# Turned blocks in a Mamba-2 / gated-MLP layer: two buffers and another order in the SSD part, landing in place in the latent part

## The chip, the cores and the metric

The kernel runs on one core of a Trainium2 chip. The metric is device time in microseconds of one execution. A comparison goes by the median of several executions; the profile is of one more execution, taken by the hardware profiler, with a time of its own.

## The reference

One layer over 256 latent tokens with a prefix of 256 context tokens, width 2048, all in float32. In short:

```
shift, scale, gate = split(silu(c) @ w_ada + b_ada)          # and the same for the context
h = rmsnorm(tokens, g_pre) * (1 + scale) + shift
z = h @ w_in              # x, B, C, dt for all 512 tokens; z_ssd, u, v, z_mlp for the 256 latents
xbc = silu(depthwise_conv5(z[:4096] channels))               # 2048 of x, 1024 of B, 1024 of C
y = bidirectional SSD scan(x, dt, A, B, C), chunks of 128, 8 groups of 4 heads;
    the latents' scans start from the context's final states
y_a = rmsnorm((y + d_skip * x) * silu(z_ssd), g_ssd)
y_b = rmsnorm(u * (w_s . rmsnorm(v, g_v) + b_s) * silu(z_mlp), g_mlp)
out = x + gate * rmsnorm(concat(y_a, y_b) @ w_out, g_post)
```

In a group of the scan, products such as `states = B^T (decay * dt * x)` contract over tokens, so x and B are needed with tokens in the partitions, while the projection leaves them with channels in the partitions: a block must be turned.

## The kernel before, in words

**Products in three parts.** Every large weight arrives as float32 and is split into hi (rounded, ScalarE) and lo = w - hi (VectorE), in halves of 128 x 1024 (lines 84 to 89; in the SSD part by `split_hi` and `split_lo`, lines 540 to 550). TensorE then does hi x hi, hi x lo and lo x hi. The pool of halves holds four hi and four lo.

**Stages.** (1) Up to about 122 us: adaLN, norms, the first seven channel tiles and dt. (2) To about 450 us: the remaining 25 of 32 channel tiles (`REST`, line 24), 48 matmuls each, of 512 columns for x and B tiles and 256 for C tiles. The tiles go by groups: of group g, tiles 4g and 4g+1 are x, 4g+2 is B, 4g+3 is C. While TensorE does later tiles, the finished ones are convolved and their group's SSD products are done. (3) To about 820 us: 16 blocks of 512 columns for the latents (v, u, z_mlp, z_ssd, four each), and what is computed from them. (4) The output projection in two halves, then the last norm and the output.

**The planner.** In stage 2 and in the first block of stage 3 the order of instructions on TensorE, VectorE, ScalarE and GpSimd is the order in which the program writes them (`manual_schedule`). Steps are written through `later(dt, fn)`, line 578, which puts a step into a queue with a due time, and `pump(dt)`, line 582, which moves the planner's clock on by dt and writes all steps that are due. `pump` is called after every six matmuls: with 1.3 for tiles of 512 columns, 0.65 for tiles of 256. So the due times decide the order and nothing else; on the chip an instruction starts when its engine is free and its inputs are there. SP, which issues the DMAs, is ordered by the framework, as are all engines from the second latent block on (line 1218 ends the manual part).

**One group in stage 2** (`plan_tile`, line 972). After a tile is done come its convolution and silu, then:
- x and B are turned, for group 0 by TensorE (`ptx`, `ptb`, into PSUM, and a copy by ScalarE) and for the others by `turn` and `turned` (lines 738 and 745): VectorE turns 32 x 32 squares into a tile T (tag `tt`, one buffer for x's two turns and B's), SP stores T to a scratch in DRAM (`Dx`, `Db`, two buffers), and four loads on SP bring it back to `xk` or `bk` with the squares in place. For group 7 B and y go by TensorE too, x does not. `LAND`, 4.5, is the time that the planner leaves for a landing.
- `ssd_w` (line 780): six products on GpSimd, x by decay and dt, into `xw` (four) and `xl` (two); `ssd_sk` two more, d_skip by x, into y, due 3 later.
- Once C is there and `late` more: `ssd_cb` (matmul `pcb`), `ssd_states` (matmuls `psc` from bk and xw, `psl` from bk and xl, lines 865 and 868), then `hs` (`ssd_hc`, `ssd_hd`, `ssd_hl`), `ssd_m`, `ssd_o` (matmul `pso`, line 917), `ssd_yo`, `ssd_ya`, `ssd_yd` (matmul `psy`). `late` is 8 for groups 1 to 6, but 10 for groups 1 and 3.
- y is turned back the same way: `ssd_yc` (T and store `Dy`), `ssd_yt` (loads into `yz`) and `ssd_yf` (line 966, VectorE adds yz to y).
- For the next group, `ssd_d`, `ssd_min` and `ssd_e` make the decay matrix E from R; after the second minimum GpSimd's queue issues the load of the next R (`row_load`, line 721).

**y** is one tile of 128 x 2 x 2048 (token half, channel). Before the scan its eight segments of 512 serve as scratch (`yseg`).

**The latents' turned blocks** (stage 3, z_mlp as kind 2 and z_ssd as kind 3). `lat_z` multiplies block j4 of `vt` or y with silu(z) and squares it for the norm. `lat_t` (line 1110) turns squares into T with VectorE and moves each square into place with 16 DMAs on GpSimd's queue, into a second tile Z; T and Z share a pool of two buffers (tag `gw`, also used by `lat_vn`). `lat_split` (line 1123) scales four parts of Z by g_mlp or g_ssd and splits them into hi and lo, for the output projection. They are due 1.5 and 17 to 20 after the block's end; a block is 20.8 long on the planner's clock.

Of the kernel before, what the change touches and what calls it, by code (L numbers as in the profile page):

```python
# [8 lines left out]
F32 = mybir.dt.float32  # L9
# [6 lines left out]
P = 128  # L16
D = 2048
# [3 lines left out]
NGRP = 8  # L21
# [26 lines left out]
def tile_hybrid_ssd_mlp(  # L48
# [46 lines left out]
    ypool = ctx.enter_context(mkpool(name="ypool", bufs=1, side="right"))  # L95
    y = ypool.tile([P, 2, D], F32, tag="big16", name="y")
    st = ExitStack()
# [56 lines left out]
    def yseg(j):  # L154
        return y[:, j // 4, (j % 4) * 512 : (j % 4 + 1) * 512]

# [8 lines left out]
    s2 = yseg(4)[:, 0:256]  # L165
    at = y[:, 0, 256:512].rearrange("p (t h) -> p t h", t=4)
    fold = yseg(7)[:, 256:320]
# [348 lines left out]
    drp = ctx.enter_context(mkpool(name="drp", bufs=1, space=bass.MemoryType.DRAM))  # L516
    drt = ctx.enter_context(mkpool(name="drt", bufs=2, space=bass.MemoryType.DRAM))
    cv1 = cvs.enter_context(mkpool(name="cv1", bufs=1))
# [216 lines left out]
    def by_pe(g, what):  # L735
        return g == 0 or g == NGRP - 1 and what != "x"

# [12 lines left out]
    def ssd_x(g, xi):  # L750
        S = gs_.setdefault(g, {})
        if xi == 0:
            S["xk"] = cv2.tile([P, 2, 4, P], F32, tag="xk", name=f"xk{g}")
        xt = done.pop(4 * g + xi)
        if not by_pe(g, "x"):
            T = cv1.tile([P, 512], F32, tag="tt", name=f"tx{g}{xi}")
            S["Dx", xi] = turn(T, xt, f"x{g}{xi}")
            return
        p = spt([P, 4, P], f"ptx{g}{xi}")
        for t in range(4):  # L760
            nc.tensor.transpose(p[:, t, :], xt[:, t * P : (t + 1) * P], ident)
        S["ptx", xi] = p

    def ssd_xc(g, xi):
        xk = gs_[g]["xk"][:, xi]
        if by_pe(g, "x"):
# [13 lines left out]
    def ssd_w(g):  # L780
        S = gs_[g]
        h4 = slice(4 * g, 4 * g + 4)
        xw = cv1.tile([P, 2, 2, 256], F32, tag="xw", name=f"xw{g}")
        for t in range(2):
            for d in range(2):
                nc.gpsimd.tensor_tensor(hx(xw[:, t, d, :]), xtok_(g, t), hb(wctx(t, d)[:, h4]), op=ALU.mult)
        xl = cv1.tile([P, 2, 256], F32, tag="xl", name=f"xl{g}")
        for d in range(2):
            nc.gpsimd.tensor_tensor(hx(xl[:, d, :]), xtok_(g, 2 + d), hb(wlt(d)[:, h4]), op=ALU.mult)
        S["xw"], S["xl"] = xw, xl  # L790

    def ssd_b(g):
        bt = done[4 * g + 2]
        S = gs_.setdefault(g, {})
        S["bk"] = cv1.tile([P, 4, P], F32, tag="bk", name=f"bk{g}")
        if not by_pe(g, "b"):
            T = cv1.tile([P, 512], F32, tag="tt", name=f"tb{g}")
            S["Db"] = turn(T, bt, f"b{g}")
            return
        p = spt([P, 4, P], f"ptb{g}")  # L800
        for t in range(4):
            nc.tensor.transpose(p[:, t, :], bt[:, t * P : (t + 1) * P], ident)
        S["ptb"] = p
# [101 lines left out]
    def yg(g, c):  # L905
        return y[:, c, g * 256 : (g + 1) * 256]

# [58 lines left out]
    def ssd_yf(g):  # L966
        ya = y[:, :, g * 256 : (g + 1) * 256]
        nc.vector.tensor_tensor(ya, ya, gs_[g]["pty"].rearrange("p c q k -> p c (q k)"), op=ALU.add)
# [83 lines left out]
    def open_lat():  # L1052
# [3 lines left out]
        gsp = gs.enter_context(mkpool(name="gsp", bufs=1))  # L1056
        L_["vt"] = L_["big"].tile([P, 2, D], F32, tag="b16", name="vt")
        L_["cb2"] = gsp.tile([P, D], F32, name="cb2")
# [51 lines left out]
    def lat_t(kind, j4):  # L1110
        src = L_["vt"] if kind == 2 else y
        cols = slice(j4 * 512, (j4 + 1) * 512)
        T = L_["lt2"].tile([P, 1024], F32, tag="gw", name=f"T{kind}{j4}").rearrange("p (t j c) -> p t j c", t=2, j=4)
        for tk in range(2):
            nc.vector.transpose(T[:, tk].rearrange("p j c -> p (j c)"), src[:, tk, cols])
        Z = L_["lt2"].tile([P, 1024], F32, tag="gw", name=f"Z{kind}{j4}")
        L_["Z"] = Z = Z.rearrange("p (t j c) -> p t j c", t=2, j=4)
        for a in range(4):
            for b in range(4):
                nc.gpsimd.dma_start(Z[32 * b : 32 * b + 32, :, :, 32 * a : 32 * a + 32].rearrange("p t j c -> p (t j) c"),  # L1120
                                T[32 * a : 32 * a + 32, :, :, 32 * b : 32 * b + 32].rearrange("p t j c -> p (t j) c"))

    def lat_split(kind, j):
        src = L_["Z"][:, :, j % 4]
        if kind == 2:
            gcol, hi, lo = C_GMLP, hhi[j][:, 0:256], hlo[j][:, 0:256]
        else:
            gcol, hi, lo = C_GSSD, L_["yah"][:, j, :], L_["yal"][:, j, :]
        hi, lo = (t.rearrange("p (t c) -> p t c", t=2) for t in (hi, lo))
        gc = pc[:, gcol + j : gcol + j + 1]  # L1130
        nc.scalar.mul(hi, src, gc)
        nc.vector.scalar_tensor_tensor(lo, src, gc, hi.bitcast(F32), op0=ALU.mult, op1=ALU.subtract)

    def lat_v(j4, pa):
        cols = slice(j4 * 512, (j4 + 1) * 512)
        for tk in range(2):
            nc.scalar.copy(L_["vt"][:, tk, cols], pa[tk])
            sqj = L_["lt2"].tile([P, 512], BF16, tag="sqj", name=f"sqv{j4}{tk}")
# [4 lines left out]
    def lat_vn(j4):  # L1143
# [5 lines left out]
        for tk in range(2):  # L1149
            vb = L_["vt"][:, tk, cols]  # L1150
            nc.vector.scalar_tensor_tensor(vb, vb, rr[:, 0, tk : tk + 1], gvb, op0=ALU.mult, op1=ALU.mult)
        L_["ws"] = ws

    def lat_sg(j4):
        ws = L_["ws"]
        L_["sg"] = []
        for tk in range(2):
            p = spt([P, 512], f"psg{j4}{tk}")
            for gi in range(4):
                g = 4 * j4 + gi  # L1160
                nc.tensor.matmul(p[:, gi * P : (gi + 1) * P], lhsT=ws[:, gi, :],
                                 rhs=L_["vt"][:, tk, g * P : (g + 1) * P], start=True, stop=True)
            L_["sg"].append(p)

    def lat_u(j4, pa):
        for tk in range(2):
# [26 lines left out]
    for blk in range(16):  # L1193
# [243 lines left out]
```

## Time and profile before

| | us |
|---|---|
| Median of three executions (976.14 to 978.86) | 978.4 |
| The profiled execution | 974.69 |
| Its span, first to last instruction | 972.8 |
| TensorE busy in it | 955.7 |
| VectorE busy | 685.6 |
| ScalarE busy | 482.8 |
| GpSimd busy | 198.6 |

In the rows of the profile, PE is TensorE's matmuls, PEld its weight loads, DVE is VectorE, ACT ScalarE, POOL GpSimd and SP the engine that issues most DMAs (SPq its queue). A row of the timeline gives start, length, engine, line, operation, output<-inputs, shape, count (a row with x4 covers four instructions in a row), and in brackets how long the engine had stood idle and what ended that. Float32 matmuls without the split count as two records each. A row of waits gives total, number and longest. Names are those of the program's tiles without their numbers, so `bk<-Db` is a load of the turned B of any group. "L549" is line 549 of the kernel before; the printed functions carry the same numbers.

### The profile page before, as it was taken

What the parts mean: (1) busy time and instruction counts of PE and PEld (TensorE: products, weight loads), DVE (VectorE), ACT (ScalarE), POOL (GpSimd) and SP (SyncE); (2) the same over time, 40 slices, a digit from 0 to 9 for tenths busy, and PEclk for the clock granted to TensorE, in tenths of its full rate; (3) what the DMA queues carried; (4) which work ended last, traced back from release to release, by engine and by line L of the source; (5) the groups of instructions that cost most, each with busy time, mean ns of one, the idle gap of its engine ahead of it and who ended that gap; (6) DMA issues with size and microseconds to landing.
All of it is one profiled execution on the core that took longest, in us unless ns stands there. A gap on an engine that the chain in (4) does not pass through costs nothing.

```text
span 972.8 us, 13786 instructions
## 1 busy us (share of the span) xinstructions
PE 955.7 (98%) x5138; PEld 771.8 (79%) x5138; DVE 685.6 (70%) x1101; ACT 482.8 (50%) x731; POOL 198.6 (20%) x290
## 2 busy tenths in 40 slices
PE   9999999998997999999999999999999999999997
PEld 4688888786785878787888888887888888888885
DVE  6888798878985868676767776767666665445636
ACT  4344458564662544455445433465565564346612
POOL 0000002522551233354000000043334541000000
PEclk9999999999999999999999999999999999999999
DMA  9999956567676666575877868686556665556722
GB/s 363 417 415 415 365 224 165 149 182 158 138 189 169 147 172 149 160 217 209 295 304 281 289 254 314 259 305 210 200 195 222 223 233 192 212 177 251 266 87 86
DMA packets 145666, 225.09 MB, mean 231 GB/s; under 512 B 114992, under 2 KB 115248, under 8 KB 122944
## 3 DMA queue, kind: packets, MB, share of 16 engines
q1 hardware_dynamic: 138816, 206.55, 62.6%
q0 software_dynamic: 6208, 16.85, 5.4%
q8 instruction: 40, 0.66, 0.3%
q10 hardware_dynamic: 576, 0.82, 0.2%
q14 instruction: 26, 0.21, 0.1%
HBM read 211.02 MB, written 8.98 MB: 226 GB/s over the span
## 4 chain that ended last, share of the span: by engine, by line
PE 87%; DMA 6%; DVE 4%; ACT 1%; SPq 1%; issue 1%; DVEq 0%; ACTq 0%
PE pa L1212 12%; PE pa L1214 12%; PE pa L1213 12%; PE psx L141 8%; PE psx L142 8%; PE psx L143 8%; PE pm L1255 3%; PE pm L1254 3%; PE pm L1253 3%; DMA ada<-in_wada_dram 3%; PE pq L1255 2%; PE pq L1254 2%; PE pq L1253 2%; PE psc L865 2%; PE pso L917 1%; DMA wst<-in_wst_dram 1%
## 5 line engine op out<-in xcount | busy, mean ns | idle before, releaser
L88 DVE TENSOR_TENSOR lo_w<-w,hi_w 128x1024 fp32r<-128x1024 f32 x173 | 210.7, 1222 | 148.8 <-ACT hi_w L87 148.7
L87 ACT CAST hi_w<-w 128x1024 fp32r<-128x1024 f32 x173 | 182.2, 1053 | 220.7 <-PE pa L1214 147.9
L1212 PE MATMUL pa<-hi_w,hhi 128*128 128x512 f32 x512 | 201.2, 393 | 0.0
L1213 PE MATMUL pa<-lo_w,hhi 128*128 128x512 f32 x512 | 199.4, 390 | 0.0
L1214 PE MATMUL pa<-hi_w,hlo 128*128 128x512 f32 x512 | 199.4, 389 | 0.0
L141 PE MATMUL psx<-hhi,hi_w 128*128 128x512 f32 (+1 forms) x400 | 151.5, 379 | 0.0
L143 PE MATMUL psx<-hhi,lo_w 128*128 128x512 f32 (+1 forms) x400 | 145.8, 364 | 0.0
L142 PE MATMUL psx<-hlo,hi_w 128*128 128x512 f32 (+1 forms) x400 | 145.7, 364 | 0.0
L1212 PEld LDWEIGHTS pa<-hi_w,hhi 128*128 128x128 f32 x512 | 96.2, 188 | 20.9 <-issue 1.6
L1214 PEld LDWEIGHTS pa<-hi_w,hlo 128*128 128x128 f32 x512 | 96.1, 188 | 20.0
L1213 PEld LDWEIGHTS pa<-lo_w,hhi 128*128 128x128 f32 x512 | 96.2, 188 | 19.8 <-issue 0.2
L624 DVE SCALAR_TENSOR_TENSOR xbc<-psx,pc,xbc 128x248 f32<-128x248 f32 (+1 forms) x204 | 83.4, 473 | 19.7 <-ACT xbc L608 19.0
L549 DVE TENSOR_TENSOR lo_w<-w,hi_w 128x1024 fp32r<-128x1024 f32 x61 | 81.8, 1349 | 20.0 <-ACT hi_w L543 20.0
L1120 POOL DMA_DIRECT2D Z<-T x128 | 73.7, 583 | 97.2 <-ACT sq L1188 33.0
L141 PEld LDWEIGHTS psx<-hhi,hi_w 128*128 128x128 f32 x400 | 75.5, 189 | 14.4 <-issue 3.1
L142 PEld LDWEIGHTS psx<-hlo,hi_w 128*128 128x128 f32 x400 | 75.6, 189 | 12.9 <-issue 1.7
L143 PEld LDWEIGHTS psx<-hhi,lo_w 128*128 128x128 f32 x400 | 75.5, 189 | 12.2
L543 ACT CAST hi_w<-w 128x1024 fp32r<-128x1024 f32 x61 | 63.6, 1045 | 42.5 <-PE psx L142 29.5
L1253 PE MATMUL pm<-hi_w,hhi 128*128 128x512 f32 x128 | 49.8, 389 | 0.0
L1255 PE MATMUL pm<-hi_w,hlo 128*128 128x512 f32 x128 | 49.8, 389 | 0.0
L1254 PE MATMUL pm<-lo_w,hhi 128*128 128x512 f32 x128 | 49.8, 389 | 0.0
L378 ACT CAST hi_st<-wst 128x448 fp32r<-128x448 f32 (+2 forms) x26 | 17.2, 679 | 57.0 <-DMA wst<-in_wst_dram 57.0
(274 smaller groups left out, 1407.6 us busy)
## 6 DMA issues: line engine op xcount, KB each, us to landing
w<-in_wlat_dram SPq DMA_DIRECT2D x64, 1024.0 KB, 4.8
w<-in_wout_dram SPq DMA_DIRECT2D x32, 1024.0 KB, 4.8
w<-in_wxbc_dram SPq DMA_DIRECT2D x25, 1024.0 KB, 5.6
ada<-in_wada_dram SPq DMA_DIRECT2D x24, 1024.0 KB, 14.0
gate<-in_wada_dram SPq DMA_DIRECT2D x16, 1024.0 KB, 5.0
ada<-in_wada_dram SPq DMA_DIRECT2D x16, 512.0 KB, 12.5
R<-acs POOLq DMA_DIRECT2D x8, 1024.0 KB, 7.0
wst<-in_wst_dram SPq DMA_DIRECT2D x15, 480.0 KB, 13.0
```

The lines of the kernel that those rows point to most:

```text
L87: nc.scalar.copy(hi, raw)
L88: nc.vector.tensor_tensor(lo, raw, hi.bitcast(F32), op=ALU.subtract)
L141: nc.tensor.matmul(ps, lhsT=whi, rhs=hhi[k][:, s], start=start, stop=False)
L142: nc.tensor.matmul(ps, lhsT=whi, rhs=hlo[k][:, s], start=False, stop=False)
L143: nc.tensor.matmul(ps, lhsT=wlo, rhs=hhi[k][:, s], start=False, stop=stop)
L624: nc.vector.scalar_tensor_tensor(ao, zi, cw[:, k : k + 1], ao, op0=ALU.mult, op1=ALU.add)
L1212: nc.tensor.matmul(pa[tk], lhsT=hhi[k][:, t], rhs=whi[:, w], start=k == 0, stop=False)
L1213: nc.tensor.matmul(pa[tk], lhsT=hhi[k][:, t], rhs=wlo[:, w], start=False, stop=False)
L1214: nc.tensor.matmul(pa[tk], lhsT=hlo[k][:, t], rhs=whi[:, w], start=False, stop=k == KT - 1)
L1253: nc.tensor.matmul(p, lhsT=yh[:, t], rhs=whi[:, w], start=j == 0, stop=False)
L1254: nc.tensor.matmul(p, lhsT=yh[:, t], rhs=wlo[:, w], start=False, stop=False)
L1255: nc.tensor.matmul(p, lhsT=yl[:, t], rhs=whi[:, w], start=False, stop=hf == 0 and j == 15)
```

## The change

Five things, by place:
- **Layout.** y and vt become 128 x 4 x 2 x 512 (block, token half, column), so that a block of 512 columns of both halves is contiguous in a partition. Every use is rewritten to the same elements.
- **SSD, buffers.** T (tag `tt`) moves to a pool of two buffers, the scratch in DRAM from two to four.
- **SSD, products.** `ssd_w` keeps the four products of xw; the two of xl become `ssd_wl`, due 3 later, and `ssd_sk` is due 6 after `ssd_w`, where x goes by DMA.
- **SSD, order.** `late` is at least 11 instead of 8 (14 for tile 15, so group 3), `ssd_yt` is due 3 later and `ssd_yf` 4 later after the y product. Of group 7, the second x tile goes by TensorE.
- **Latents.** The 16 DMAs write into the block they came from; Z is gone. The four scales of a block are copied into a small tile first, over a copy of four columns of the newest weight half; the splits read scales from there and are due 23 to 23.3 after the block's end.

```diff
-    y = ypool.tile([P, 2, D], F32, tag="big16", name="y")
+    y = ypool.tile([P, 4, 2, 512], F32, tag="big16", name="y")
...
     def yseg(j):
-        return y[:, j // 4, (j % 4) * 512 : (j % 4 + 1) * 512]
+        return y[:, j % 4, j // 4]
...
-    drt = ctx.enter_context(mkpool(name="drt", bufs=2, space=bass.MemoryType.DRAM))
+    drt = ctx.enter_context(mkpool(name="drt", bufs=4, space=bass.MemoryType.DRAM))
...
     def by_pe(g, what):
-        return g == 0 or g == NGRP - 1 and what != "x"
+        return g == 0 or g == NGRP - 1 and what != "x0"
...
-        if not by_pe(g, "x"):
-            T = cv1.tile([P, 512], F32, tag="tt", name=f"tx{g}{xi}")
+        if not by_pe(g, f"x{xi}"):
+            T = cv2.tile([P, 512], F32, tag="tt", name=f"tx{g}{xi}")
...
+        S["xw"] = xw
+
+    def ssd_wl(g):
+        h4 = slice(4 * g, 4 * g + 4)
         xl = cv1.tile([P, 2, 256], F32, tag="xl", name=f"xl{g}")
         for d in range(2):
             nc.gpsimd.tensor_tensor(hx(xl[:, d, :]), xtok_(g, 2 + d), hb(wlt(d)[:, h4]), op=ALU.mult)
-        S["xw"], S["xl"] = xw, xl
+        gs_[g]["xl"] = xl
...
-            T = cv1.tile([P, 512], F32, tag="tt", name=f"tb{g}")
+            T = cv2.tile([P, 512], F32, tag="tt", name=f"tb{g}")
...
-        lx, lb, ly = (0.7 if by_pe(g, w) else LAND for w in "xby")
+        lx, lb, ly = (0.7 if by_pe(g, w) else LAND for w in (f"x{r}", "b", "y"))
         if lx == LAND:
             tw = max(tw, 2 * LAND + 3)
         if lb == LAND:
-            late = max(late, 8.0)
+            late = max(late, 14.0 if i == 15 else 11.0)
...
         if r == 1:
+            late_w = lx == LAND
             later(d0 + tx + tw, lambda: ssd_w(g))
-            later(d0 + tx + tw + 3, lambda: ssd_sk(g))
+            later(d0 + tx + tw + (3 if late_w else 0), lambda: ssd_wl(g))
+            later(d0 + tx + tw + (6 if late_w else 3), lambda: ssd_sk(g))
...
-                          (16.9 + td + (1.7 if ly < 1 else LAND), ssd_yt), (18.6 + td + (0.7 if ly < 1 else 2 * LAND + 2), ssd_yf)]:
+                          (16.9 + td + (1.7 if ly < 1 else LAND + 3), ssd_yt), (18.6 + td + (0.7 if ly < 1 else 2 * LAND + 6), ssd_yf)]:
...
     def lat_t(kind, j4):
-        src = L_["vt"] if kind == 2 else y
-        cols = slice(j4 * 512, (j4 + 1) * 512)
-        T = L_["lt2"].tile([P, 1024], F32, tag="gw", name=f"T{kind}{j4}").rearrange("p (t j c) -> p t j c", t=2, j=4)
+        src = (L_["vt"] if kind == 2 else y)[:, j4]
+        T = L_["lt2"].tile([P, 1024], F32, tag="gw", name=f"T{kind}{j4}").rearrange("p (u c) -> p u c", c=P)
         for tk in range(2):
-            nc.vector.transpose(T[:, tk].rearrange("p j c -> p (j c)"), src[:, tk, cols])
-        Z = L_["lt2"].tile([P, 1024], F32, tag="gw", name=f"Z{kind}{j4}")
-        L_["Z"] = Z = Z.rearrange("p (t j c) -> p t j c", t=2, j=4)
+            nc.vector.transpose(T[:, 4 * tk : 4 * tk + 4].rearrange("p u c -> p (u c)"), src[:, tk])
+        dst = src.rearrange("p t (j c) -> p (t j) c", c=P)
         for a in range(4):
             for b in range(4):
-                nc.gpsimd.dma_start(Z[32 * b : 32 * b + 32, :, :, 32 * a : 32 * a + 32].rearrange("p t j c -> p (t j) c"),
-                                T[32 * a : 32 * a + 32, :, :, 32 * b : 32 * b + 32].rearrange("p t j c -> p (t j) c"))
+                nc.gpsimd.dma_start(dst[32 * b : 32 * b + 32, :, 32 * a : 32 * a + 32],
+                                    T[32 * a : 32 * a + 32, :, 32 * b : 32 * b + 32])
 
     def lat_split(kind, j):
-        src = L_["Z"][:, :, j % 4]
+        src = (L_["vt"] if kind == 2 else y)[:, j // 4, :, (j % 4) * P : (j % 4 + 1) * P]
+        if j % 4 == 0:
+            L_["gc"] = L_["lt2"].tile([P, 4], F32, tag="gc", name=f"gc{kind}{j}")
+            gcol = (C_GMLP if kind == 2 else C_GSSD) + j
+            nc.vector.tensor_copy(L_["gc"], halves[max(halves)][0][:, 0:4].bitcast(F32))
+            nc.vector.tensor_copy(L_["gc"], pc[:, gcol : gcol + 4])
...
-        gc = pc[:, gcol + j : gcol + j + 1]
+        gc = L_["gc"][:, j % 4 : j % 4 + 1]
         nc.scalar.mul(hi, src, gc)
         nc.vector.scalar_tensor_tensor(lo, src, gc, hi.bitcast(F32), op0=ALU.mult, op1=ALU.subtract)
...
             for jj in range(4):
-                later(17 + jj, lambda kind=kind, j=4 * j4 + jj: lat_split(kind, j))
+                later(23 + 0.1 * jj, lambda kind=kind, j=4 * j4 + jj: lat_split(kind, j))
```

More of the change, by code (lines that the diff above doesn't have):

```diff
@@ L165, in tile_hybrid_ssd_mlp @@
     s2 = yseg(4)[:, 0:256]
-    at = y[:, 0, 256:512].rearrange("p (t h) -> p t h", t=4)
+    at = yseg(0)[:, 256:512].rearrange("p (t h) -> p t h", t=4)
     fold = yseg(7)[:, 256:320]
@@ L765, in ssd_xc @@
         xk = gs_[g]["xk"][:, xi]
-        if by_pe(g, "x"):
+        if by_pe(g, f"x{xi}"):
             nc.scalar.copy(xk, gs_[g]["ptx", xi])
@@ L905, in yg @@
     def yg(g, c):
-        return y[:, c, g * 256 : (g + 1) * 256]
+        return y[:, g // 2, c, (g % 2) * 256 : (g % 2 + 1) * 256]
     def ssd_sk(g):
@@ L966, in ssd_yf @@
     def ssd_yf(g):
-        ya = y[:, :, g * 256 : (g + 1) * 256]
+        ya = y[:, g // 2, :, (g % 2) * 256 : (g % 2 + 1) * 256]
         nc.vector.tensor_tensor(ya, ya, gs_[g]["pty"].rearrange("p c q k -> p c (q k)"), op=ALU.add)
@@ L1056, in open_lat @@
         gsp = gs.enter_context(mkpool(name="gsp", bufs=1))
-        L_["vt"] = L_["big"].tile([P, 2, D], F32, tag="b16", name="vt")
+        L_["vt"] = L_["big"].tile([P, 4, 2, 512], F32, tag="b16", name="vt")
         L_["cb2"] = gsp.tile([P, D], F32, name="cb2")
@@ L1110, in lat_t @@
     def lat_t(kind, j4):
[L1111 to L1113 removed]
+        src = (L_["vt"] if kind == 2 else y)[:, j4]
+        T = L_["lt2"].tile([P, 1024], F32, tag="gw", name=f"T{kind}{j4}").rearrange("p (u c) -> p u c", c=P)
         for tk in range(2):
[L1115 to L1117 removed]
+            nc.vector.transpose(T[:, 4 * tk : 4 * tk + 4].rearrange("p u c -> p (u c)"), src[:, tk])
+        dst = src.rearrange("p t (j c) -> p (t j) c", c=P)
         for a in range(4):
             for b in range(4):
[L1120 to L1121 removed]
+                nc.gpsimd.dma_start(dst[32 * b : 32 * b + 32, :, 32 * a : 32 * a + 32],
+                                    T[32 * a : 32 * a + 32, :, 32 * b : 32 * b + 32])
     def lat_split(kind, j):
[L1124 removed]
+        src = (L_["vt"] if kind == 2 else y)[:, j // 4, :, (j % 4) * P : (j % 4 + 1) * P]
[4 more added lines that the diff above has]
+            nc.vector.tensor_copy(L_["gc"], pc[:, gcol : gcol + 4])
         if kind == 2:
[L1126 removed]
+            hi, lo = hhi[j][:, 0:256], hlo[j][:, 0:256]
         else:
[L1128 removed]
+            hi, lo = L_["yah"][:, j, :], L_["yal"][:, j, :]
         hi, lo = (t.rearrange("p (t c) -> p t c", t=2) for t in (hi, lo))
[L1130 removed]
+        gc = L_["gc"][:, j % 4 : j % 4 + 1]
         nc.scalar.mul(hi, src, gc)
@@ L1134, in lat_v @@
     def lat_v(j4, pa):
-        cols = slice(j4 * 512, (j4 + 1) * 512)
         for tk in range(2):
-            nc.scalar.copy(L_["vt"][:, tk, cols], pa[tk])
+            nc.scalar.copy(L_["vt"][:, j4, tk], pa[tk])
             sqj = L_["lt2"].tile([P, 512], BF16, tag="sqj", name=f"sqv{j4}{tk}")
@@ L1149, in lat_vn @@
         for tk in range(2):
-            vb = L_["vt"][:, tk, cols]
+            vb = L_["vt"][:, j4, tk]
             nc.vector.scalar_tensor_tensor(vb, vb, rr[:, 0, tk : tk + 1], gvb, op0=ALU.mult, op1=ALU.mult)
@@ L1161, in lat_sg @@
                 nc.tensor.matmul(p[:, gi * P : (gi + 1) * P], lhsT=ws[:, gi, :],
-                                 rhs=L_["vt"][:, tk, g * P : (g + 1) * P], start=True, stop=True)
+                                 rhs=L_["vt"][:, j4, tk, gi * P : (gi + 1) * P], start=True, stop=True)
             L_["sg"].append(p)
@@ L1172, in lat_u @@
                 s = slice(gi * P, (gi + 1) * P)
-                nc.vector.scalar_tensor_tensor(L_["vt"][:, tk, g * P : (g + 1) * P], p[:, s],
+                nc.vector.scalar_tensor_tensor(L_["vt"][:, j4, tk, s], p[:, s],
                                                pc[:, C_BS + g : C_BS + g + 1], ub[:, s], op0=ALU.add, op1=ALU.mult)
     def lat_z(kind, j4, pa):
-        src = L_["vt"] if kind == 2 else y
-        cols = slice(j4 * 512, (j4 + 1) * 512)
+        src = (L_["vt"] if kind == 2 else y)[:, j4]
         if kind == 3 and j4 == 0:
@@ L1184, in lat_z @@
             nc.scalar.activation(sz, pa[tk], AF.Silu)
-            tb = src[:, tk, cols]
+            tb = src[:, tk]
             nc.vector.tensor_tensor(tb, tb, sz, op=ALU.mult)
```

## The prediction

> **What bounds the kernel.** I read the page first, then the waits of TensorE, then its busy time in stretches of 25 us, and then went into the two stretches that stand out. The page gives the span and the share of TensorE:
>
> ```profile
> span 972.8 us, 13786 instructions
> PE 955.7 (98%) x5138; PEld 771.8 (79%) x5138; DVE 685.6 (70%) x1101; ACT 482.8 (50%) x731; POOL 198.6 (20%) x290
> ```
>
> TensorE is the bound, so only three things count: its idle time, instructions that run slower than usual on it, and instructions added to it. Its waits between 122 and 940 us are one line:
>
> ```profile
> PE psc L865 <- DMA bk<-Db: 8.3, 2, 5.2
> ```
>
> Two waits, 8.3 us together, both in front of ssd_states, both for the turned B (bk). The stretches show where, beside an undisturbed one (columns: length; busy us and instructions of PE, PEld, DVE, ACT, POOL; granted clock; DMA share; GB/s):
>
> ```profile
> 225.00:250.00 25.00, 21.85 (x92) 16.73 (x91) 20.83 (x40) 11.27 (x21) 9.98 (x12) 1.00 0.69 176
> 300.00:325.00 25.00, 19.83 (x85) 14.29 (x85) 16.87 (x37) 9.62 (x23) 5.08 (x5) 0.93 0.53 133
> 825.00:850.00 25.00, 25.00 (x112) 20.71 (x111) 11.50 (x10) 9.49 (x9) 0.00 (x0) 1.00 0.53 190
> ```
>
> The idle time is 25 - 21.85 = 3.15 us and 25 - 19.83 = 5.17 us. After the longer one the clock was 0.93 over the stretch. The last row gives the pace: 25 / 112 = 0.223 us a matmul of 512 columns, so one planner step (six of them, 1.3 on its clock) is 1.34 us. The chain of waits shows what the slower clock cost, and what a turn on TensorE costs:
>
> ```profile
> 145.29 0.44 PE ptx L761 x4
> ...
> 238.45 1.95 PE psc L865 x4
> ...
> 305.21 3.43 PE psc L865 x4
> ...
> 351.41 1.72 PE psc L865 x4
> ```
>
> The same four records (two matmuls) take 1.72 us undisturbed, 1.95 after the first wait, and 3.43 after the second. Together that is 0.23 + 1.71 = 1.94 us beside the waits.
>
> The Trainium skill, "TensorE: Matmul & The Clock Gate", Part 1, says that the clock drops to half after an idle window of about 3.4 us. The rows agree: twice the duration after 5.17 us, nearly none after 3.15. By that rule a wait that remains, but under 3.4 us, costs only itself; the sum below stands on the rows alone.
>
> **SSD: later products of B.** The planner only sets the order in which each engine's instructions stand; nothing waits for its clock. For groups 1 to 6, `late` goes from 8 to 11 (group 1 from 10 to 11, group 3 from 10 to 14). On the grid of 1.3, ssd_states of group 2 was due 8 + 6 after its last tile, which ends at 6 x 10.4 + 2 x 5.2 = 72.8 on the planner's clock: at 86.8, so at 87.1; now at 89.8, so at 91.0. That is three steps, 3 x 1.34 = 4.0 us of weight matmuls put ahead of it. Group 4 goes from 133.9 to 137.8, also three steps. Moved work costs TensorE nothing: the same matmuls run in another order. From the rows above, TensorE reached the products at 238.45 - 3.15 = 235.3 and at 305.21 - 5.17 = 300.04. Four us later is 239.3 against data at 238.45: group 2 waits for nothing even if nothing else improves. Group 4 comes at 304.0 against 305.21: 1.2 us at most stay by that alone, if the rest of that group's chain moves along with TensorE.
>
> **SSD: two buffers of T.** What brings B late in group 2 (VectorE, then the DMA issues of SP):
>
> ```profile
> 228.21 0.70 DVE L739 STREAM_TRANSPOSE tb<-xbc 128x512 f32<-128x512 f32 x1
> ...
> 232.72 0.71 DVE L739 STREAM_TRANSPOSE tx<-xbc 128x512 f32<-128x512 f32 x1 [2.85 <-DMA Db<-tb]
> ```
>
> ```profile
> 228.94 0.38 SPq L741 DMA_DIRECT2D Db<-tb  x1
> ...
> 233.47 0.36 SPq L741 DMA_DIRECT2D Dx<-tx  x1
> 233.94 2.62 SPq L747 DMA_DIRECT2D bk<-Db  x4
> ```
>
> VectorE stood 2.85 us because x's T had to wait until B's was read, and SP issued bk's loads behind x's store. With a second buffer x turns at once, its store leaves some 3 us sooner, and bk's loads start when Db lands, 1 us sooner. VectorE is not the bound, so the 2.85 us count only through this.
>
> **SSD: the products in pieces, and what they meet.** In group 4 (VectorE, GpSimd, SP):
>
> ```profile
> 289.34 4.98 DVE L549 TENSOR_TENSOR lo_w<-w,hi_w 128x1024 fp32r<-128x1024 f32 x1
> 294.24 0.70 DVE L739 STREAM_TRANSPOSE tb<-xbc 128x512 f32<-128x512 f32 x1
> 294.87 1.18 DVE L549 TENSOR_TENSOR lo_w<-w,hi_w 128x1024 fp32r<-128x1024 f32 x1
> 303.00 0.69 DVE L968 TENSOR_TENSOR y<-y,yz 128x512 f32<-128x512 f32 x1 [6.95 <-DMA yz<-Dy]
> ```
>
> ```profile
> 288.01 0.59 POOL L725 DMA_DIRECT2D R<-acs  x1 [2.21 <-issue]
> 288.62 2.33 POOL L786 TENSOR_TENSOR xw<-xk,ed 128x256 f32<-128x256 f32 x4
> ...
> 292.06 1.17 POOL L910 TENSOR_TENSOR y<-xk,dsk 128x256 f32<-128x256 f32 x2
> ```
>
> ```profile
> 296.39 2.27 SPq L747 DMA_DIRECT2D yz<-Dy  x4
> 298.85 4.16 SPq L747 DMA_DIRECT2D bk<-Db  x4
> ```
>
> While GpSimd ran eight products without a gap (288.62 to 293.23), a weight split on VectorE took 4.98 us instead of 1.18, and B's turn stood 3.8 us behind it. Then SP issued four loads of yz ahead of bk's.
>
> The pieces alone change little. xw, xl and sk are due 3 apart now, but from group 2 on no other GpSimd instruction falls between them, and GpSimd starts each as soon as its inputs are there. What changes is the order around them. Group 3 moves by three steps, so its two minima, and the row load of line 725 behind which GpSimd reaches xw of group 4, are due at 123.5 instead of 118.95. B's turn is still due at 122.2: it now comes ahead of them. yz of group 3 is due at 130.0 instead of 123.5, behind bk's loads at 126.1. So B's turn loses the 3.8 us and bk's loads lose the 2.3 us of yz. Against at most 1.2 us to go, I take group 4's wait as gone too.
>
> The Trainium skill, "SBUF — State Buffer", Who interferes with whom, lets a two-input VectorE instruction lose to a GpSimd one only for that one instruction's length. The trace does not bear that out for a run of eight. By that rule the time would be the second rival's.
>
> **SSD: one turn more on TensorE.** x1 of group 7 is turned by TensorE (0.44 us, above) and copied by ScalarE, where it went by VectorE and DMA. That is the only work added to the bound. Leaving those engines is worth nothing, since neither is the bound there.
>
> **The latents.** Z goes, and the 16 DMAs of a block write into the block itself. Same count, same pieces. The four splits of a block stand six planner units later, behind a hold: two tiny copies on VectorE a block, the first reading the newest weight half. Rows of now, by engine:
>
> ```profile
> ACT hi_w L87 <- PE pa L1214: 147.9, 93, 3.5
> ```
>
> ```profile
> 686.97 7.47 POOL L1120 DMA_DIRECT2D Z<-T  x13 [14.48 <-ACT sq L1188]
> 695.66 1.73 POOL L1120 DMA_DIRECT2D Z<-T  x3 [1.22 <-DMA Z<-T]
> ```
>
> ```profile
> 701.72 1.71 ACT L1131 ACTIVATE hhi<-Z,pc 128x256 fp32r<-128x256 f32 x4
> ```
>
> ScalarE waits for TensorE to give weight buffers back (147.9 us, 93 times), never the reverse: TensorE has three halves in hand, 3 x 12 x 0.223 = 8.0 us, and that hides the copies. The DMAs already stand behind the square that reads the block (14.48 us), so writing in place adds no wait that isn't there. Later splits give landing more time. In the undisturbed stretch above TensorE is full, so nothing can be gained. Bounds: below, no gain, as there is no idle time; above, a stand beyond 8.0 us, which is a rival. I take 0.
>
> **The sum.** On the profiled execution (972.8 span, 974.69 with what lies around it): -3.15 - 5.17 - 0.23 - 1.71 + 0.44 = -9.8, so 964.9. The median of the three runs, 978.4, stands 3.7 above that execution. I take the same 9.8 off it: **968.6**. If those 3.7 us are longer waits of the same kind, up to 3.7 more goes.
>
> **Rivals.**
>
> *One wait stays.* TensorE no longer stands 3.4 us at group 2, so VectorE loses that time to catch up before group 4. If it needed it, bk of group 4 comes up to 3.4 us later against TensorE, and 1.2 + 3.4 = 4.6 is near the old wait. Also, in group 3 the second product's input was ready just in time:
>
> ```profile
> 265.65 2.26 POOL L789 TENSOR_TENSOR xl<-xk,ed 128x256 f32<-128x256 f32 x2
> ```
>
> ```profile
> 268.10 1.03 PE L868 MATMUL psl<-xl,bk 128*128 128x256 f32 x4
> ```
>
> It ended at 267.91, 0.2 us ahead. Priced by the longest wait and its clock: 5.17 + 1.71 = 6.9, so at most 975.5.
>
> *B's turn stays late.* The products are one run on GpSimd as before, so that part of the change does not do what its name says. If the split of 4.98 us was held by something else than that run, B's turn in group 4 keeps its 3.8 us, bk lands as now, and 1.2 us of the wait stay: 968.6 + 1.2 = 969.8. For it speaks that group 2's loss needs no such hold to be explained; against it, that this one ended 1.1 us after the run did. The rule of the skill quoted above leads here.
>
> *The latents give it back.* If in-place landing held the splits beyond the 8.0 us in hand by 1.2 us in each of eight blocks, 9.6 us go: 978.2, no change. Against it: the splits ran at 701.72 with no wait for Z, and are now later.
>
> *Slower: yf stands ahead of the states.* yf of group 3 (VectorE waits for yz) was due 6.5 before hl of group 4; now it is at 139.1 and hl at 140.4, one step; likewise yf of group 6 (237.9) and hl of group 7 (239.2). TensorE's next product needs hl, and the margin is thin:
>
> ```profile
> 357.99 0.99 DVE L887 TENSOR_TENSOR hs<-psl,hs 128x256 f32<-128x256 f32 x2 [0.51 <-POOL hs L881]
> ```
>
> ```profile
> 360.64 1.88 PE L917 MATMUL pso<-hs,xbc 128*128 128x512 f32 x4
> ```
>
> 360.64 - 358.98 = 1.66 us. A stand as yf's 6.95 above would cost 6.95 - 1.66 + 1.71 = 7.0 us at each place: 968.6 + 14.0 = 982.6. It decides from yz landing more than 1.66 us after VectorE reaches yf. Against it: the loads stand 139.1 - 130.0 = 9.1 ahead of yf, 9.4 us, where 7.8 stood before, and yz's loads land in less (median 5.0 us, longest 8.5):
>
> ```profile
> DMA to landing us min/median/max: 2.1/5.0/8.5
> ```
>
> **Chances.** Both waits go, 968.6 (own range 964 to 972): 0.68. B's turn stays late, 969.8: 0.05. One wait stays, 972 to 975.5: 0.11. Latents or the like cancel it, about 978: 0.10. Slower, 982.6: 0.06. The range runs from 963.5 (the forecast less 3.7, less half the 2.7 us between the three runs) to 975.5 (one wait kept); it leaves out the last two cases, 0.16. About 0.3% (2.9 us) can be told from no change, so faster means under 975.5: 0.68 + 0.05 + 0.11 = 0.84, within 0.10, slower 0.06.
>
> **What would show it.** Right: no wait of psc for bk among TensorE's waits, a clock of 1.00 from 200 to 450, eight products of psc near 1.72, no tx waiting for Db, tb of group 4 ahead of the row load and not behind a split of 5 us, four more ptx records, about 0 of ScalarE and VectorE waiting for landings in the latents, span near 963. Wrong: any new line of TensorE waiting for xl, hs or a weight half, or a span above 968.

## The result and the profile after

| | before | changed |
|---|---|---|
| Median of six executions each, us | 977.23 (976.14 to 978.86) | 968.41 (968.11 to 969.59) |
| Profiled execution, us | 974.69 | 968.23 |
| Its span, us | 972.8 | 966.5 |

The ratio is 0.9911, 95% interval [0.9898, 0.9923]: 8.8 us faster. In the changed kernel the lines from 787 on are shifted by 4 to 9; `psc` is now L869, `psl` L872, `pso` L921, `psy` L947, `pcb` L852, `yf` L972.

The busy time of the engines:

```profile
PE 954.9 (99%) x5142; PEld 771.1 (80%) x5142; DVE 686.7 (71%) x1116; ACT 482.2 (50%) x732; POOL 192.5 (20%) x290
```

TensorE is still the bound, with the four more records of the added turn. Its waits between 122 and 960 us (total, number, longest), and the two stretches in which they stand, beside one of the latents (columns as before):

```profile
PE psc L869 <- DMA bk<-Db: 2.8, 2, 1.4
PE psx L141 <- DVE xbc L624: 0.2, 1, 0.2
```

```profile
225.00:250.00 25.00, 23.58 (x101) 18.43 (x100) 24.19 (x46) 11.29 (x21) 3.76 (x5) 1.00 0.55 106
300.00:325.00 25.00, 23.65 (x118) 18.25 (x117) 19.93 (x39) 13.37 (x27) 8.29 (x9) 1.00 0.90 209
460.00:820.00 360.00, 360.00 (x1615) 297.12 (x1614) 243.67 (x304) 184.26 (x245) 76.29 (x133) 1.00 0.72 251
```

The two waits for bk are still there, but 1.4 us each instead of 3.15 and 5.17, and the clock is full. VectorE is busy for 24.19 of 25 us in the first stretch, where it was 20.83: it is close behind TensorE there. In the latents TensorE has no idle time at all. The products themselves on TensorE:

```profile
240.72 1.96 PE L869 MATMUL psc<-xw,bk 128*128 128x512 f32 x4 [1.42 <-DMA bk<-Db]
303.66 1.95 PE L869 MATMUL psc<-xw,bk 128*128 128x512 f32 x4 [1.35 <-DMA bk<-Db]
```

What happens ahead of them. Group 2 on VectorE, on GpSimd and in SP's queue:

```profile
220.44 6.08 DVE L624 SCALAR_TENSOR_TENSOR xbc<-y,pc,xbc 128x248 f32<-128x248 f32 x8
230.62 0.71 DVE L739 STREAM_TRANSPOSE tb<-xbc 128x512 f32<-128x512 f32 x1
231.25 0.67 DVE L739 STREAM_TRANSPOSE tx<-xbc 128x512 f32<-128x512 f32 x1
```

```profile
220.19 3.04 POOL L786 TENSOR_TENSOR xw<-xk,ed 128x256 f32<-128x256 f32 x4 [6.25 <-DMA xk<-Dx]
...
224.69 1.54 POOL L914 TENSOR_TENSOR y<-xk,dsk 128x256 f32<-128x256 f32 x2
```

```profile
231.36 0.38 SPq L741 DMA_DIRECT2D Db<-tb  x1
234.46 2.30 SPq L747 DMA_DIRECT2D bk<-Db  x4
```

The turn of x (`tx`) follows B's (`tb`) with no stand between them, and bk's loads leave 3.1 us after B's store, where it was 5.0. But tb comes at 230.62, where it came at 228.21: the eight taps of the convolution ahead of it, which have two inputs in SBUF like the split, took 6.08 us beside GpSimd's products. In the kernel before, the same taps took 3.22 us, and the products came behind them:

```profile
220.53 3.22 DVE L624 SCALAR_TENSOR_TENSOR xbc<-y,pc,xbc 128x248 f32<-128x248 f32 x8
225.44 3.32 POOL L786 TENSOR_TENSOR xw<-xk,ed 128x256 f32<-128x256 f32 x4 [11.17 <-PE psx L143]
```

It is the later due times that brought the products there. With them x's turn comes ahead of y's, and x's loads leave at 213.77, ahead of yz's, where they left at 220.59, behind them. In all kernels below with `late` at 11 (order alone, one buffer and so on) the products start at 219.4 to 220.5 us and these taps take 6.08 or 6.09 us. With `late` at 8 the products start at 224.9 to 225.6, with 13 at 223.1 to 223.5, and the taps take 3.22 or 3.23. The pieces of the products still run back to back.

Group 4 on VectorE, GpSimd and in SP's queue:

```profile
287.95 1.22 DVE L549 TENSOR_TENSOR lo_w<-w,hi_w 128x1024 fp32r<-128x1024 f32 x1
289.08 0.70 DVE L739 STREAM_TRANSPOSE tb<-xbc 128x512 f32<-128x512 f32 x1
306.08 0.71 DVE L972 TENSOR_TENSOR y<-y,yz 128x512 f32<-128x512 f32 x1 [0.63 <-DMA yz<-Dy]
```

```profile
291.86 0.59 POOL L725 DMA_DIRECT2D R<-acs  x1 [2.09 <-DVE E L828]
```

```profile
289.81 0.38 SPq L741 DMA_DIRECT2D Db<-tb  x1
291.20 1.40 SPq L81 DMA_DIRECT2D w<-in_wxbc_dram  x1
292.90 6.00 SPq L747 DMA_DIRECT2D bk<-Db  x4
```

B's turn is 5.2 us earlier (294.24 before), ahead of R's load and behind a split of normal length; yz's loads are behind bk's (at 299.00). But from B's store to the product it now takes 303.66 - 289.81 = 13.9 us, where it took 305.21 - 294.97 = 10.2: the loads of bk stand beside R's load of 1 MB, and their issue takes 6.00 us, not 4.16.

### The profile page after: what moved, and what is told of

It is laid out like the page before. It is cut to its first block, busy times and chain, and to the rows that moved or that the text cites. A ratio compares the mean times of both kernels' runs of the same rounds, so it can differ in the third digit from the quotient of the medians.

```text
span 966.5 us, 13778 instructions
## 1 busy us (share of the span) xinstructions
PE 954.9 (99%) x5142; PEld 771.1 (80%) x5142; DVE 686.7 (71%) x1116; ACT 482.2 (50%) x732; POOL 192.5 (20%) x290
## 4 chain that ended last, share of the span: by engine, by line
PE 83%; DVE 7%; DMA 5%; issue 1%; SPq 1%; POOL 1%; ACT 1%; DVEq 0%; POOLq 0%; ACTq 0%
PE pa L1219 12%; PE pa L1220 12%; PE pa L1221 12%; PE psx L141 7%; PE psx L142 6%; PE psx L143 6%; PE pm L1260 3%; PE pm L1261 3%; PE pm L1262 3%; DMA ada<-in_wada_dram 3%; DVE xbc L624 3%; PE pq L1262 2%; PE pq L1260 2%; PE pq L1261 2%; PE psada L254 2%
## 5 line engine op out<-in xcount | busy, mean ns | idle before, releaser
L88 DVE TENSOR_TENSOR lo_w<-w,hi_w 128x1024 fp32r<-128x1024 f32 x173 | 210.5, 1222 | 138.1 <-ACT hi_w L87 137.9
L549 DVE TENSOR_TENSOR lo_w<-w,hi_w 128x1024 fp32r<-128x1024 f32 x61 | 76.8, 1265 | 19.7 <-ACT hi_w L543 19.6
L1124 POOL DMA_DIRECT2D y<-T x64 | 36.8, 583 | 47.8 <-ACT sq L1195 33.1
L1124 POOL DMA_DIRECT2D vt<-T x64 | 36.8, 584 | 47.3 <-ACT sq L1195 34.8
## 6 DMA issues: line engine op xcount, KB each, us to landing
ada<-in_wada_dram SPq DMA_DIRECT2D x24, 1024.0 KB, 13.9
```

Source lines behind the costliest of these rows:

```text
L88: nc.vector.tensor_tensor(lo, raw, hi.bitcast(F32), op=ALU.subtract)
```

## The experiments

The theory after the result: the gain is the time that TensorE stood for bk, and it takes both the later products and T's second buffer, because a stand of VectorE that TensorE's own wait used to hide now reaches TensorE. Rivals: the order alone does it; the latents have a share; the pieces have a share. Each kernel's ratio is to the kernel before on the same chip (medians there 976.5 to 977.2 us).

### The order of the products alone

```diff
-            late = max(late, 8.0)
+            late = max(late, 14.0 if i == 15 else 11.0)
```

> The kernel before with nothing but the later products of B (late at least 11, 14 for tile 15). Theory A (the three steps of weight matmuls put ahead of the products are what removes the waits, the buffers and pieces add little): TensorE reaches the products of group 2 at about 239.3 us and of group 4 at about 304 us, B is there as before, so at most 1.2 us of waits stay and the time is about 8 to 9 us below before, near 968 to 970. Theory B (the buffers of T and the order on VectorE are needed as well, because VectorE's lag moves along): waits of 3 us or more stay in front of psc and the gain is 5 us or less, 972 or above.

Measured: 973.43 us, ratio 0.9976 [0.9959, 0.9993]. TensorE's waits in the same window, a row of VectorE at group 2 and one ahead of group 4's hl:

```profile
PE psc L865 <- DMA bk<-Db: 3.0, 2, 2.0
PE psx L141 <- DVE xbc L624: 1.7, 2, 1.2
PE psy L943 <- DVE E L903: 1.1, 1, 1.1
PE pso L917 <- DVE hs L887: 0.9, 1, 0.9
```

```profile
235.72 0.71 DVE L739 STREAM_TRANSPOSE tx<-xbc 128x512 f32<-128x512 f32 x1 [3.39 <-DMA Db<-tb]
309.75 0.69 DVE L968 TENSOR_TENSOR y<-y,yz 128x512 f32<-128x512 f32 x1 [2.98 <-DMA yz<-Dy]
```

The wait for bk shrinks to 3.0 us, but waits for VectorE appear (3.7 us together: for xbc at 220.0 and 335.0 us, for hs at 252.5, for E at 323.1), and VectorE itself stands for T (3.39) and for yz (2.98). That is a third of the gain by the medians, a quarter by the ratio: the order alone isn't it.

### Two buffers of T alone

The kernel before, with the pool of T and the scratch as in the change:

```diff
-    drt = ctx.enter_context(mkpool(name="drt", bufs=2, space=bass.MemoryType.DRAM))
+    drt = ctx.enter_context(mkpool(name="drt", bufs=4, space=bass.MemoryType.DRAM))
...
-            T = cv1.tile([P, 512], F32, tag="tt", name=f"tb{g}")
+            T = cv2.tile([P, 512], F32, tag="tt", name=f"tb{g}")
```

> The kernel before with T in two buffers and four scratches in DRAM and nothing else. Theory B: the wait of group 2 shrinks by 1 to 2 us, the wait of group 4 stays near 5 us with the slow clock after it, since the split held beside GpSimd's run is untouched; 974 to 976. Rival: the buffers alone bring more than half of the gain, 972 or below.

Measured: 976.42 us, ratio 0.9997 [0.9985, 1.001]; TensorE's waits for bk:

```profile
PE psc L865 <- DMA bk<-Db: 7.4, 2, 4.9
```

0.9 us of the wait go and the time doesn't move, a little above the 974 to 976 that were expected.

### All but the two buffers

The same lines undone in the changed kernel:

```diff
-    drt = ctx.enter_context(mkpool(name="drt", bufs=4, space=bass.MemoryType.DRAM))
+    drt = ctx.enter_context(mkpool(name="drt", bufs=2, space=bass.MemoryType.DRAM))
...
-            T = cv2.tile([P, 512], F32, tag="tt", name=f"tb{g}")
+            T = cv1.tile([P, 512], F32, tag="tt", name=f"tb{g}")
```

> The changed kernel with T back in one buffer and two scratches in DRAM, all else as changed. Theory B (after late_only: the later products pay only if VectorE does not lose its 3 us at x's turn of group 3, because that lag reaches TensorE as other waits): VectorE waits about 3 us for Db again, and the time is 971 to 973. Theory A (the order alone): 968 to 969.

Measured: 972.31 us, ratio 0.9951 [0.9935, 0.9966], 3.9 above the changed kernel's median. The waits of TensorE, and the one of VectorE for T:

```profile
PE psc L869 <- DMA bk<-Db: 3.4, 2, 1.9
PE pso L921 <- ACT R L821: 1.4, 1, 1.4
```

```profile
DVE tx L739 <- DMA Db<-tb: 3.8, 1, 3.8
```

So the buffers are worth 0 alone and 3.9 us beside the rest of the change.

### The SSD part without the latents, and the latents without the SSD part

The first is the kernel before with the SSD changes (buffers, products, order, x1 of group 7) and the old layout; the second is the changed kernel with these undone. Of the first, the lines of the order:

```diff
-            late = max(late, 8.0)
+            late = max(late, 14.0 if i == 15 else 11.0)
```

and of the second, the same line the other way:

```diff
-            late = max(late, 14.0 if i == 15 else 11.0)
+            late = max(late, 8.0)
```

> The kernel before with the whole SSD part of the change and the old layout and latents. Theory A (the latents give nothing, because TensorE is full there): 968.4 within 1 us, the time of the changed kernel. Rival C (the latents carry part of the gain): 970 or above.

> The changed kernel with the whole SSD part undone: only the layout of y and vt, landing in place, the scales that hold the splits and their later place. Theory A: the time of before within 1 us (977.2), with the two waits for bk in front of psc as before. Rival C: 975 or below. Rival D (the latents cost something that the SSD part pays for): 978.5 or above.

Measured: the SSD part alone 969.73 us, ratio 0.9929 [0.991, 0.9947], between its two forecasts; the layout and latents alone 976.32, ratio 1.0 [0.9988, 1.0011], with the old waits for bk (8.2 us, two, the longest 5.3).

By themselves the latents give nothing and cost nothing, within the interval of some 1.1 us. The 1.3 us between the SSD part alone and the whole are not told from nothing, as the two intervals overlap; a small share beside the SSD part is neither shown nor excluded.

### The products in one piece

The changed kernel with `ssd_w` and `ssd_sk` as before:

```diff
-            later(d0 + tx + tw + (3 if late_w else 0), lambda: ssd_wl(g))
-            later(d0 + tx + tw + (6 if late_w else 3), lambda: ssd_sk(g))
+            later(d0 + tx + tw + 3, lambda: ssd_sk(g))
```

> The changed kernel with xl's products back behind xw's and the skip's products due 3 later, as before. Theory N (the pieces stand in the same order on GpSimd from group 2 on, so they change nothing): 968.4 within 1 us. Rival P (the pieces part the run of eight and so shorten what VectorE loses): 970 or above, and longer lo_w splits beside the products.

Measured: 969.37 us, ratio 0.9929 [0.9912, 0.9946]; TensorE waits 3.2 us for bk instead of 2.8. At most about 1 us, not told from nothing.

### y's loads and sum at their old due times

```diff
-(16.9 + td + (1.7 if ly < 1 else LAND + 3), ssd_yt), (18.6 + td + (0.7 if ly < 1 else 2 * LAND + 6), ssd_yf)]:
+(16.9 + td + (1.7 if ly < 1 else LAND), ssd_yt), (18.6 + td + (0.7 if ly < 1 else 2 * LAND + 2), ssd_yf)]:
```

> The changed kernel with y's loads and y's last sum due as before (4.5 after the turn, and 11 instead of 15 after). Theory Y (in late_only VectorE stood 3.0 us for yz ahead of hl of group 4, and TensorE then waited 0.9 for hs, 1.1 for E and 1.7 for a free bank): VectorE stands 2 to 3 us for yz again, 969.5 to 971.5. Rival: 968 to 969, nothing of it reaches TensorE once T has two buffers.

Measured: 970.04 us, ratio 0.9928 [0.9911, 0.9946]. TensorE's waits for VectorE, and VectorE's for yz:

```profile
PE psx L141 <- DVE xbc L624: 1.5, 2, 1.2
PE psy L947 <- DVE E L907: 0.9, 1, 0.9
```

```profile
DVE y L972 <- DMA yz<-Dy: 2.8, 1, 2.8
```

Some 1.6 us by the medians; the intervals overlap, but no execution of either kernel (969.62 to 970.52, and 968.11 to 969.59) lies among the other's. The later `ssd_yf` keeps a stand of 2.8 us away from VectorE. VectorE carries it along (the taps of xbc behind it start at 327.59 us, and at 324.82 in the changed kernel), and it reaches TensorE in 1.5 + 0.9 = 2.4 us of waits where the changed kernel has 0.2. Of the waits that the expectation names for the order alone, the 0.9 us for hs stand at 252.5 us, long before VectorE's stand for yz, and don't come of it; E's and the longer one for xbc come behind it.

### Products later still; R's load later; both

`late` 13 and 16 instead of 11 and 14:

```diff
-            late = max(late, 14.0 if i == 15 else 11.0)
+            late = max(late, 16.0 if i == 15 else 13.0)
```

and R's load for group 5 taken from behind the second minimum and made due 8.3 later:

```diff
-        if c == 1:
+        if c == 1 and g != 4:
...
+            if g == 4:
+                later(d0 + 9, lambda: row_load(g + 1))
```

> The changed kernel with late at least 13 instead of 11 (16 for tile 15): one or two steps more of weight matmuls, 1.3 to 2.7 us, ahead of each group's products. Theory A: the two waits of 1.4 us that are left go, 965.5 to 967. Theory B (VectorE's lag reaches TensorE at another place): waits for xbc, hs or E take their place, 968 or above.

> The changed kernel with one DMA moved: the load of the next R in group 4 (1 MB, on GpSimd's queue) is due 8.3 later, so behind B's loads. Theory R (in the changed kernel B of group 4 took 13.8 us from store to landing because this load ran beside it): store to landing at most 9 us, the wait of group 4 (1.35 us) gone, group 2's 1.4 us unchanged, 967 within 1 us. Rival W (the weight load just ahead on SP's queue slows it): the wait stays, 968.4.

> Both edits: late at least 13 and the load of R in group 4 behind B's loads. No wait for B left and VectorE's order as in the changed kernel: 965.5 to 966.5. Rival: R then comes too late for ScalarE's adds of group 5 and holds its queue, 968 or above.

Measured: 968.34 us (0.9912 [0.9898, 0.9927]), 968.66 (0.9914 [0.99, 0.9929]) and 968.47 (0.9915 [0.9902, 0.9928]): none differs from the changed kernel, and the forecasts of 965.5 to 967 all missed. With products later still, alone or with R's load later, no wait for bk is left; in its place stands

```profile
PE pso L921 <- DVE hs L891: 2.8, 5, 0.6
```

five waits of up to 0.6 us for VectorE's states, the same 2.8 us. The later due time doesn't take R's load away from bk's: a due time orders GpSimd's queue and holds nothing back. SP's, GpSimd's and TensorE's rows of group 4 in that run:

```profile
293.01 2.24 SPq L747 DMA_DIRECT2D bk<-Db  x4
```

```profile
294.60 0.59 POOL L725 DMA_DIRECT2D R<-acs  x1
```

```profile
303.60 3.20 PE L871 MATMUL psc<-xw,bk 128*128 128x512 f32 x4 [1.99 <-DMA bk<-Db]
```

R leaves 0.65 us before the last of bk's four issues ends (295.25), and the product waits 1.99 us, no less than in the changed kernel. That leaves R's part open; the next run asks in another way.

### R's load in SP's queue, behind the loads of B and y

As above, and the load itself:

```diff
-        nc.gpsimd.dma_start(R.rearrange("p h d c q -> p (h d c q)"),
+        (nc.sync if g == 5 else nc.gpsimd).dma_start(R.rearrange("p h d c q -> p (h d c q)"),
```

> The changed kernel with the load of R for group 5 (1 MB) issued on SP's queue, behind B's and y's loads of group 4, instead of on GpSimd's queue ahead of the products; in row_later that load still left at 294.6 us, beside B's, because nothing held it there. Theory R (this load beside B's small ones is what stretches them): B of group 4 is there by about 299 to 300 us, the wait of group 4 is gone, the 1.4 us of group 2 stay, 967 within 1 us. Rival W (the 1 MB weight load just ahead of B's loads on SP's queue stretches them): B comes at 302 us or later and the wait stays, 968.4 or more.

Measured: 968.3 us, ratio 0.9912 [0.9896, 0.9927]. SP's queue at group 4, the product, and all waits of TensorE between 122 and 960 us:

```profile
292.95 2.19 SPq L747 DMA_DIRECT2D bk<-Db  x4
300.42 0.34 SPq L725 DMA_DIRECT2D R<-acs  x1
```

```profile
301.75 1.88 PE L871 MATMUL psc<-xw,bk 128*128 128x512 f32 x4
```

```profile
PE psc L871 <- DMA bk<-Db: 1.5, 1, 1.5
PE psx L141 <- DVE xbc L624: 1.2, 1, 1.2
PE psy L949 <- DVE E L909: 0.3, 1, 0.3
```

With R's load out of the way group 4's product waits for nothing. The issue of bk's loads took as long in the run before this one (2.24 us, and 2.19 here), the weight load ahead of them stayed where it was, and there the product waited; so it is the landing of bk beside R's load that was late, not the issue. The tile's view has the landings of these four loads, here in the changed kernel:

```profile
DMA to landing us min/median/max: 5.2/9.6/10.0
```

The median is 7.8 us with R's load later, 5.8 with it on SP's queue and 2.4 in the kernel before. So R's load is what made TensorE wait, but the second rival has a share too: 5.8 is not 2.4, and the weight load left 1.7 us ahead of bk's loads, where it was 3.5 in the kernel before (the last section has the other rows). The time stays the same all the same: 1.2 and 0.3 us of waits for VectorE come up instead.

### Ten products in a row on GpSimd

The kernel before; in group 4 the two products of d_skip are done twice, with the same values:

```diff
-        for c in range(2):
+        for c in (0, 1, 0, 1) if g == 4 else (0, 1):
```

> The kernel before with the two skip products of group 4 done twice (the same values written again), so that GpSimd's run beside the weight split of 4.98 us has ten products instead of eight, 1.2 us more. If a split waits until GpSimd's whole run is over, it now takes about 6.2 us, and the wait of group 4 grows from 5.2 to about 6.4 us. If it waits for one GpSimd instruction only and lost its 3.8 us to something else, it stays at 5 us or less.

Measured in one execution: 979.24 us. The split on VectorE, the last products on GpSimd, and TensorE's wait:

```profile
292.40 6.13 DVE L549 TENSOR_TENSOR lo_w<-w,hi_w 128x1024 fp32r<-128x1024 f32 x1
```

```profile
295.12 2.32 POOL L910 TENSOR_TENSOR y<-xk,dsk 128x256 f32<-128x256 f32 x4
```

```profile
PE psc L865 <- DMA bk<-Db: 10.1, 2, 6.3
```

Two products more (1.16 us) make the split 1.15 us longer (4.98 to 6.13), and it again ends 1.1 us after the run does (298.53 against 297.44). So this split was held until the whole run was over, and with it B's turn. The Trainium skill, "SBUF — State Buffer", Who interferes with whom, gives a VectorE instruction only the one GpSimd instruction to wait for; the two lengths speak against that here.

It is no rule for all such instructions. In group 2 of the kernel before, a split that began 1.3 us into a run of eight products ended long before the run (231.49):

```profile
226.73 1.56 DVE L549 TENSOR_TENSOR lo_w<-w,hi_w 128x1024 fp32r<-128x1024 f32 x1
```

There GpSimd lost the time, 3.32 us for four products that took 2.33 in group 4. And the eight taps of 6.08 us in the changed kernel took turns with the products, 0.82 us for a tap and 0.79 for a product. What decides which of the two waits, and for how long, stays open.

## Why the prediction was right, step by step

- **The bound and the place: right.** The SSD part moves the time; the latents alone are worth 0, as taken, and TensorE is busy for all 360.00 us from 460 to 820. The added turn is there (four records, 0.44 us).
- **Later products: right for TensorE.** At group 2 TensorE came to the product at 240.72 - 1.42 = 239.3, the predicted 239.3. At group 4 it came at 303.66 - 1.35 = 302.3; the predicted 304.0 stood on the clock of before, with group 2's wait in it.
- **"Group 2 waits for nothing even if nothing else improves": wrong, by 1.42 us.** It set TensorE's new arrival against bk's old landing, 238.45. But bk became ready at 240.72, 2.3 us later. B's turn comes 2.4 us later, behind taps that ran beside GpSimd's products, and it is the new order itself that put the products there. What the second buffer won behind B's store (3.1 instead of 5.0 us) was lost in the landing of bk's loads, 5.0 us instead of 2.6, with a weight load 1.7 us ahead of them instead of 4.5 (last section). The first rival named a lag of VectorE, but at group 4, and as time in which it could not catch up; this one arises at 220 us, ahead of TensorE's first wait.
- **Group 4's wait gone: wrong, by 1.35 us.** B's turn lost its cover as predicted (289.08 instead of 294.24, a split of 1.22 instead of 4.98) and yz's loads went behind. Not in the sum was that the row load, though put behind B's turn, would run beside bk's loads; from store to product it took 13.9 - 10.2 = 3.7 us more than before. The run with R on SP's queue shows that R's load made the wait: without it beside them the wait was gone.
- **The sum: mis-sized, and by two terms of opposite sign.** In the profiled executions the waits fell by 8.3 - 2.8 - 0.2 = 5.3 us, not 8.3; the slow products by 1.94 - 0.24 - 0.23 = 1.5, not 1.94; with the turn, -5.3 - 1.5 + 0.44 = -6.4 against a span 6.3 shorter, where -9.8 was predicted. The median fell by 8.8 all the same. The profiled execution of before was a good one, 2.5 us under the median of its six; that of the changed kernel is at its median. The prediction allowed that such a distance might go too, as longer waits. The profile of the kernel with the latents alone, whose SSD part is that of before and whose 976.31 us are closer to the usual time, shows that it isn't longer waits but a slower clock after them:

```profile
237.62 2.65 PE L865 MATMUL psc<-xw,bk 128*128 128x512 f32 x4 [2.89 <-DMA bk<-Db]
240.06 1.91 PE L868 MATMUL psl<-xl,bk 128*128 128x256 f32 x4
306.17 3.75 PE L865 MATMUL psc<-xw,bk 128*128 128x512 f32 x4 [5.29 <-DMA bk<-Db]
309.72 1.39 PE L868 MATMUL psl<-xl,bk 128*128 128x256 f32 x4
```

  Against the profiled execution of before (1.95 and 3.43, and 1.03 for psl, the duration it has in the prediction's rows too) that is 0.70 + 0.88 + 0.32 + 0.36 = 2.3 us more, at waits of 8.2 us as there. (It is one execution, and its span is only 1.6 us longer; what else in it is shorter was not followed.) The granted clocks say the same for many: of 60 further executions of the kernel before, the ten with a mean of 0.997, as in the profiled one, have a median of 974.5 us, and the 24 with 0.994 one of 976.8; the changed kernel's are at 0.998 and 0.999. So 968.6 came out near 968.41 because 3.4 us too much were taken from the waits and the products, and 2.5 too little for what the usual execution of before loses beyond the profiled one, from a start 1.2 us too high (978.4, with 977.23 the median of six). That three errors cancel to 0.2 us is luck.
- **The pieces change little: right** (at most 1 us).
- **"The 2.85 us count only through this": wrong.** The prediction let VectorE's stand for T count only through bk's loads leaving 1 us sooner, as VectorE is not the bound. With the rest of the change the second buffer is worth 3.9 us. Without it VectorE stands 3.8 us, and TensorE waits longer for bk at group 2 (1.94 instead of 1.42), runs its products there slower (2.39 + 1.91 instead of 1.96 + 1.03) and waits 1.4 us for R at 252.1.
- **The slower rival** did not come: in group 4 `ssd_yf` stands 0.63 us for yz, where it was 6.95. With `ssd_yf` at its old due time it stood 2.8 to 3.0 us, behind which TensorE waited, as this rival meant, but 2.1 to 2.3 us in all and not 7.0.

What stays open: the share of the order beside everything else isn't measured. The changed kernel with `late` as before, and with the products of xl and sk back in their places, has no time, because instructions written in that order deadlock.

## What to carry to other kernels

A new order that takes a wait from the bounding engine moves the arrival of the data too: here it brought GpSimd's products beside the taps ahead of B's turn, and R's load beside B's. And the engine behind loses the wait that hid its own stands. So price the new arrival, not the old one, and look for the next wait on the bounding engine. Here the versions that took the remaining 2.8 us away, or half of it, got about as much back as waits for VectorE and stayed at 968.3 to 968.5 us. Two parts can each be worth little alone and much together (3 and 0 us, and 7 to 9 in the kernels that have both; these two with nothing else were not run), so an edit that gives nothing by itself may still be the one that is missing. Set one profiled execution beside the median of many before a sum is taken from it: a kernel whose bounding engine waits long enough to lose its clock differs from itself by several us.

## What the runs showed of the hardware

**The clock after short waits.** The prediction cited the Trainium skill, "TensorE: Matmul & The Clock Gate", Part 1, for a wait under some 3.4 us costing only itself. The rows speak against this reading. With the order alone, after a wait of only 1.97 us, and in the changed kernel with one buffer after 1.94, the products took:

```profile
241.67 2.91 PE L865 MATMUL psc<-xw,bk 128*128 128x512 f32 x4 [1.97 <-DMA bk<-Db]
244.37 1.81 PE L868 MATMUL psl<-xl,bk 128*128 128x256 f32 x4
```

```profile
240.80 2.39 PE L869 MATMUL psc<-xw,bk 128*128 128x512 f32 x4 [1.94 <-DMA bk<-Db]
242.98 1.91 PE L872 MATMUL psl<-xl,bk 128*128 128x256 f32 x4
```

that is 1.5 to 2 us more than 1.72 and 1.03 (and the row of 1.99 us with R's load later, 3.20, is of the same kind), with the granted clock at 0.93 in that stretch, while 3.15 us cost 0.23 in the profiled execution of before, 2.16 cost 0.24 with the SSD part alone (at group 4), and the waits of 1.35 and 1.42 in the changed kernel cost some 0.24 each. That page of the Trainium skill calls the window free-running, which fits that the length alone does not decide; that waits as short as 1.94 us can cost the clock is what the runs add.

**Small loads beside large ones.** Four loads of 64 KB each, turned blocks from the scratch in DRAM, were used 13.9 us after the block's store with R's load of 1 MB on GpSimd's queue beside them, and 1.35 us of that the product stood waiting; with R behind them on SP's queue it found them there. Their issue took 6.00, 2.24 and 2.19 us in three runs, and the second waited like the first: the time of the issue doesn't tell when such loads land. Their landing does. Over the profiled executions of all 14 kernels, groups 2 and 4, the median of four, us:

| Weight load (1 MB) ahead of bk's loads by | R's load (1 MB) | cases | landing of bk's loads |
|---|---|---|---|
| 3.2 or more | none, or 4 or more ahead | 13 | 2.3 to 2.7 |
| 1.0 to 1.7 | none, or 3.4 or more behind | 10 | 4.8 to 5.8 |
| 1.7 | from 1.1 ahead to 1.6 behind | 5 | 7.8 to 9.8 |

No run moved the weight load by itself, so the first two rows only compare kernels that differ in more. Between the second row and the third there is a pair in which nothing but R's load moved: 7.8 with it 1.6 us behind bk's loads, 5.8 with it 7.5 behind.
